# A two-layer attention and long-convolution kernel on one core: 512-column q/k/v products, softmax weights scaled ahead of their transposes, first transfers alternating, raw weights fetched ahead of slots, and a program order planned with other paces

## The chip, the core and the metric

The kernel runs on one core of a Trainium2 chip, as one launch. The metric is the device time of that launch in microseconds (us). The profile names the engines PE (TensorE, with PEld for its weight loads), DVE (VectorE), ACT (ScalarE), POOL (GpSimd) and SP (SyncE, which here only issues transfers).

## What is computed

Two layers of a diffusion backbone over 512 latent tokens and 256 context tokens, width 1024, all in float32. Cut to what matters:

```python
for layer in range(2):
    mod, mod_c = silu(c) @ w_mod + b_mod, silu(c_ctx) @ w_mod + b_mod   # six shifts, scales, gates
    h = rms_norm(x, norm_mix) * (1 + scale1) + shift1                   # h_ctx the same, by mod_c
    q, k, v, hy, g = split(h @ w_in)             # 8 query heads, 2 key/value heads of 128, 1536, 2048
    q, k = rope(head_norm(q)), rope(head_norm(k))
    p = softmax(q @ keys.T * 128**-0.5)          # latents see 256 context and 512 latent keys
    attn = p @ vals
    hyo = long_conv(short_conv(hy)) ...          # by DFT; filters from a small sine MLP
    merged = sigmoid(g_a) * (attn @ w_o_attn) + sigmoid(g_h) * (hyo @ w_o_hyena)
    x = x + gate1 * (merged @ w_out)
    x = x + gate2 * swiglu(rms_norm(x) * (1 + scale2) + shift2)
return rms_norm(x, norm_final)
```

In layer 0 the context tokens pass through everything; in layer 1 only their keys and values are needed.

## The kernel before, in words

Activations lie transposed, as eight tiles of 128 features by 768 tokens (512 latents, then 256 context). Each operand of a large product is kept as two float32r tiles, a high part and the rest, and `mm3` (L233) makes a product of three matmuls: high by high, high by low, low by high. Weights come as raw tiles of 512 KB (`w_load`, L330); ACT copies the high part, DVE subtracts for the low one. Slots are fixed (`SLOTS`): 5 raw, 4 high, 4 low, 37 of 768 columns ("s"; short-lived use is asked for as "t"), 13 of 1024 columns ("f"), 8 PSUM banks ("ps").

**Order.** No engine's order is written by hand. Generators (`job`, `attn_part`, `norm`, ...) yield what their next step needs. `Order` (L65) keeps a clock for each engine, adds a rough cost for every instruction, and lets that generator go on which can and has the lowest priority number. What is emitted is the program order of each engine, and on the chip each engine runs its own row strictly in that order.

**Stages.**

- Front: a filter MLP of three layers (`filter_mlp`, L609), whose seven DVE instructions are emitted with each of its products; 32 float32 products of the conditioning with `wmodf` (`mod_first`, L390), in 16 tiles of 512 KB, which give the columns `mod`; squares of the residual, summed (`Sums`, L466), then `rms` (L486: products with ones, a root on DVE, transposes of `ny`), then `norm` (L511), eight feature tiles, two DVE steps each. `program` (L1217) puts transfers on SP's queue: a tile of `wmodf`, and those of x between them by `X_AT`, then those of the context, then weights.
- Hyena columns (`Hyena.cols`, L797), filters and convolutions (by DFT tables).
- q, k, v by `tok_chunk` (L916): tokens are the stationary side, 256 columns of weights are streamed. k, v and four pairs of query heads are six chunks, each with two weight tiles of 4 x 128 rows by 256 columns.
- Attention by `attn_part` (L1021): a unit is one head and 256 queries. Scores, maximum, exponential with its sum, transposes of the unscaled weights in blocks of 128, product with v into `O`; the reciprocal `ri` is then spread over 128 columns by two transposes, copied by ACT, multiplied into `O` by DVE, and split in high and low. 24 units in layer 0 (16 on latents, 8 on context), 16 in layer 1. Gate products run between them.
- Merge, output projection, feed-forward in four groups. At the end of layer 0 the down projection goes by three parts of 256 tokens (`END`); each part is normed for layer 1 while the next is multiplied.

The model's prices that the change touches:

```python
cost = n / 2400 + 0.003 if n >= 192 else 0.213          # mm, float32r
od.run("DMA" if n > 1 << 16 else q, n / 360e3, ...)      # dma
```

Of the kernel before, what the change touches and what calls it, by code (L numbers as in the profile page):

```python
# [19 lines left out]
P = 128  # L20
# [44 lines left out]
class Order:  # L65
    """Puts the work of several generators into one program order.

    A generator yields what its next step needs: tiles that were written, free
    slots ("tag", n) or Events. Rough costs of the instructions emitted so far
    say when these are there; of the generators that can go on, the one with  # L70
    the lowest priority number does.
    """
# [7 lines left out]
    @staticmethod  # L80
    def span(ap):
        step = ap.ap[0][0]
        lo = ap.offset % step if step else ap.offset
        return ap.tensor.name, lo, lo + 1 + sum((n - 1) * abs(st) for st, n in ap.ap[1:])
# [16 lines left out]
    def run(self, eng, cost, outs, ins, late=0.15, born=None, after=0.0):  # L101
        start = max(self.now[eng], after)
        if born is not None:
            start = max(start, self.born.get(born.tensor.name, 0.0))
        for ap in ins:
            if ap.tensor.name in self.writes:
                start = max(start, self.after(ap, eng))
        for ap in outs:
            start = max(start, self.born.get(ap.tensor.name, 0.0))
        end = start + cost  # L110
        self.now[eng] = end
        for ap in ins:
            n = ap.tensor.name
# [13 lines left out]
    def give(self, tag, i, tile_):  # L127
        self.free[tag].append((self.used.get(tile_.tensor.name, 0.0), i))
# [45 lines left out]
LANES, MORE_LANES = (2, 5), (0, 3)  # L174
# [4 lines left out]
START = 2  # L179
# [8 lines left out]
SLOTS = {"raw": 5, "hi": 4, "lo": 4, "s": 37, "f": 13, "ps": 8}  # L188


def hyena_body(ctx, tc, I, out):
# [7 lines left out]
    # ------------------------------------------------------------- tiles and instructions  # L199
    def new(tag, dt=F32, n=None):  # L200
# [71 lines left out]
    def dma(o, i, eng=None):  # L272
# [4 lines left out]
        od.run("DMA" if n > 1 << 16 else q, n / 360e3, [o], [i], late=2.0, after=od.now[q])  # L277
# [10 lines left out]
    def rsqrt(y, u):  # L288
        """y becomes (u / RS) ** -0.5."""
# [37 lines left out]
    loaded, at = {}, [0, 0]  # L327
    w_here = [Event() for _ in plan]

    def w_load(src, nk, nf, one=False):  # L330
        n = nk * nf
        raw = new("raw")
        if one:
# [5 lines left out]
        loaded[at[1]] = [x.rearrange("p (k f) -> p k f", k=nk) for x in (hi, lo)] + [tiles]  # L339
        w_here[at[1]].set = True  # L340
        raw_n = raw[:, 0:n]
        dma(raw_n.rearrange("p (k f) -> p k f", k=nk), src, nc.sync)
        yield [raw_n]
# [1233 lines left out]
```

## Time and profile before

| | |
|---|---|
| time, median of 3 runs | 2189.53 us (2187.34 to 2191.62) |
| span of the profiled execution | 2187.6 us |
| what lies around the span in that execution | not in the profile; the median stands 1.9 us above the span |
| DMA, mean over the span | 117 GB/s |
| ACT busy | 34% |

The span runs from the first to the last instruction in the trace. A share of busy time is the union of an engine's instructions; matmuls overlap, so a busy PE hides gaps shorter than a matmul's latency. How fast PE really goes is read from the count of matmuls in a stretch without gaps.

### The profile page before, as it was taken

What the parts mean: (1) busy time and instruction counts of PE and PEld (TensorE: products, weight loads), DVE (VectorE), ACT (ScalarE), POOL (GpSimd) and SP (SyncE); (2) the same over time, 40 slices, a digit from 0 to 9 for tenths busy, and PEclk for the clock granted to TensorE, in tenths of its full rate; (3) what the DMA queues carried; (4) which work ended last, traced back from release to release, by engine and by line L of the source; (5) the groups of instructions that cost most, each with busy time, mean ns of one, the idle gap of its engine ahead of it and who ended that gap; (6) DMA issues with size and microseconds to landing.
All of it is one profiled execution on the core that took longest, in us unless ns stands there. A gap on an engine that the chain in (4) does not pass through costs nothing.

```text
span 2187.6 us, 31896 instructions
## 1 busy us (share of the span) xinstructions
PE 2146.5 (98%) x12849; PEld 1888.5 (86%) x12849; DVE 1365.3 (62%) x2510; ACT 744.3 (34%) x1350; POOL 116.8 (5%) x218
## 2 busy tenths in 40 slices
PE   7999999999999999999999999999999999999997
PEld 2889999999888888888888887899888898888887
DVE  5879766665796799733333477766756666434345
ACT  3432234444522421121221334224455443222222
POOL 2111100000100000000000011200001000000000
PEclk9999999999999999999999999999999999999999
DMA  9334521112465257812112232522213433323221
GB/s 327 100 117 151 192 81 46 37 51 80 152 229 183 78 196 239 306 44 74 65 50 82 102 111 91 182 85 73 102 49 121 158 111 99 106 83 111 80 95 57
DMA packets 83060, 256.84 MB, mean 117 GB/s; under 512 B 10668, under 2 KB 15183, under 8 KB 82912
## 3 DMA queue, kind: packets, MB, share of 16 engines
q1 hardware_dynamic: 63840, 197.43, 26.7%
q0 software_dynamic: 19072, 57.36, 8.0%
q8 instruction: 101, 1.65, 0.3%
q14 instruction: 47, 0.39, 0.1%
HBM read 232.07 MB, written 22.68 MB: 116 GB/s over the span
## 4 chain that ended last, share of the span: by engine, by line
PE 92%; DVE 4%; issue 2%; ACT 1%; DMA 1%; POOL 0%; SPq 0%; DVEq 0%; ACTq 0%; POOLq 0%
PE ps L230 89%; PE ps L240 3%; DVE s L250 1%; DVE f L254 1%; ACT s L244 1%; DVE s L254 1%; DMA s<-gated 0%; DVE mx L265 0%; DVE lo L254 0%; DMA s<-in_fw 0%; DMA f<-in_wmodf 0%; ACT hi L244 0%; ACT f L244 0%; POOL s L273 0%; DVE ss L265 0%
## 5 line engine op out<-in xcount | busy, mean ns | idle before, releaser
L230 PE MATMUL ps<-s,hi 128*128 128x512 f32 (+1 forms) x4288 | 1136.2, 353 | 7.5 <-ACT s L244 3.6
L230 PEld LDWEIGHTS ps<-s,hi 128*128 128x128 f32 x4288 | 748.5, 190 | 113.9 <-ACT s L244 4.9
L230 PE MATMUL ps<-s,lo 128*128 128x512 f32 (+1 forms) x2144 | 751.6, 351 | 1.0 <-DVE lo L254 1.0
L230 PEld LDWEIGHTS ps<-s,lo 128*128 128x128 f32 x2144 | 406.5, 190 | 55.5 <-DVE lo L254 1.4
L244 ACT ACTIVATE hi<-raw 128x1024 fp32r<-128x1024 f32 (+2 forms) x272 | 267.3, 994 | 354.1 <-PE ps L230 217.7
L254 DVE TENSOR_TENSOR lo<-raw,hi 128x1024 fp32r<-128x1024 f32 (+2 forms) x272 | 308.0, 1142 | 48.8 <-ACT hi L244 46.8
L230 PE MATMUL ps<-f,hi 128*128 128x512 f32 (+1 forms) x1184 | 297.0, 341 | 0.0
L250 DVE SCALAR_TENSOR_TENSOR s<-s,ps 128x512 f32<-128x512 f32 (+1 forms) x184 | 107.0, 587 | 280.1 <-ACT s L244 150.4
L244 ACT ACTIVATE s<-ps 128x512 f32<-128x512 f32 (+5 forms) x228 | 107.9, 492 | 353.5 <-PE ps L230 273.8
L230 PEld LDWEIGHTS ps<-f,hi 128*128 128x128 f32 x1184 | 205.0, 190 | 25.4
L230 PE MATMUL ps<-f,lo 128*128 128x512 f32 (+1 forms) x592 | 201.4, 340 | 0.0
L230 PE MATMUL ps<-hi,s 128*128 128x256 f32 x1024 | 191.6, 285 | 0.4 <-ACT s L244 0.4
L250 DVE SCALAR_TENSOR_TENSOR s<-ps,mod,s 128x256 f32<-128x256 f32 (+1 forms) x144 | 83.1, 586 | 154.2 <-PE ps L230 154.0
L230 PEld LDWEIGHTS ps<-hi,s 128*128 128x128 f32 x1024 | 162.0, 192 | 0.6 <-ACT s L244 0.6
L230 PE MATMUL ps<-f 128*128 128x256 f32 (+1 forms) x1014 | 145.5, 290 | 7.5 <-DMA f<-in_fw 3.9
L244 ACT ACTIVATE f<-ps 128x512 fp32r<-128x512 f32 (+2 forms) x164 | 90.2, 585 | 170.0 <-PE ps L230 127.2
L230 PE MATMUL ps<-lo,s 128*128 128x256 f32 x512 | 144.9, 283 | 0.0
L230 PEld LDWEIGHTS ps<-f 128*128 128x128 f32 (+1 forms) x1014 | 131.0, 190 | 12.4 <-DVE f L254 4.4
L244 ACT ACTIVATE s<-ps,nb 128x256 f32<-128x256 f32 (+1 forms) x144 | 80.7, 567 | 146.4 <-DVE nb L259 142.5
L244 ACT ACTIVATE s<-s 128x256 f32<-128x256 f32 (+4 forms) x161 | 76.6, 484 | 157.7 <-DVE s L250 125.3
L230 PEld LDWEIGHTS ps<-f,lo 128*128 128x128 f32 x592 | 112.2, 189 | 12.6
L254 DVE TENSOR_TENSOR f<-ps,f 128x512 fp32r<-128x512 f32 (+2 forms) x144 | 90.2, 654 | 41.2 <-ACT f L244 40.2
(119 smaller groups left out, 1858.9 us busy)
## 6 DMA issues: line engine op xcount, KB each, us to landing
raw<-in_w_gu SPq DMA_DIRECT2D x88, 512.0 KB, 3.3
raw<-in_wmodt SPq DMA_DIRECT2D x80, 512.0 KB, 4.3
raw<-in_w_down SPq DMA_DIRECT2D x48, 384.0 KB, 3.1
raw<-in_w_gate SPq DMA_DIRECT2D x32, 512.0 KB, 3.4
raw<-in_w_hy SPq DMA_DIRECT2D x24, 512.0 KB, 4.4
raw<-in_w_qkv SPq DMA_DIRECT2D x24, 512.0 KB, 3.3
raw<-in_w_out SPq DMA_DIRECT2D x24, 512.0 KB, 3.2
f<-in_tab POOLq DMA_DIRECT2D x40, 256.0 KB, 5.6
```

The lines of the kernel that those rows point to most:

```text
L230: nc.tensor.matmul(out=o, lhsT=l, rhs=r, start=start, stop=stop)
L240: nc.tensor.transpose(o, x, ident[0:n, 0:n])
L244: nc.scalar.activation(out=o, in_=i, func=f, **kw)
L250: nc.vector.scalar_tensor_tensor(out=o, in0=a, scalar=s, in1=b, op0=op0, op1=op1)
L254: nc.vector.tensor_tensor(out=o, in0=a, in1=b, op=op)
```

## The change

- `tok_chunk` streams 512 columns. k and v of both heads are one chunk, the queries two chunks of four heads; a weight tile is 2 x 128 rows by 512 columns. A chunk goes through the tokens in two halves of 3 tiles (2 in layer 1's queries), with as many PSUM banks at once, and holds four weight tiles.
- `attn_part`: after the exponential and `ri`, DVE multiplies both weight tiles by `ri`; the two transposes of `ri`, ACT's copy and DVE's product at the end go; ACT and DVE split `O` from PSUM, in a generator of its own.
- Front: a tile of `wmodf` and one of x alternate, then a tile of `wmodf` and one of the context; four weights are asked for after the eighth pair. The first hyena columns of layer 0 take three weights at once. The filter stage is a generator of its own.
- Weights: a raw tile may be fetched when fewer than 6 weights are under way, not only when a high and a low slot are free.
- The model: 0.0135 for 0.003 us per matmul, half the price for small float32 products, 400 for 360 GB/s. Priorities, the number of attention lanes and the placing of gate products differ.

```diff
-LANES, MORE_LANES = (2, 5), (0, 3)
+LANES, MORE_LANES = (2, 10), (4, 5)
-X_AT = (2, 5, 8, 10, 12, 13, 14, 15)
-CONV, SPEC, TURN, ROPE, LANE, HYP, NORM2, LONG, STORE, SPLIT = -7, 1, 4, 2, 4, -7, 2, 3, 3, -5
+FIRST_W, AHEAD = 4, 2
+CONV, SPEC, TURN, ROPE, LANE, HYP, NORM2, LONG, STORE, SPLIT = -3, 3, 4, -1, 4, -10, 4, 3, 4, -5
-MIX = ((2, 0, 1, 0), (0, 1, 0, 0))
-EARLY = (5, 3)
+MIX = ((4, 2, 2, 1), (3, 2, 2, 1))
...
-            cost = n / 2400 + 0.003 if n >= 192 else 0.213
+            cost = n / 2400 + 0.0135 if n >= 192 else 0.213
...
-    def w_load(src, nk, nf, one=False):
+    def w_load(i, src, nk, nf, one=False):
...
+        raw_n = raw[:, 0:n]
+        dma(raw_n.rearrange("p (k f) -> p k f", k=nk), src, nc.sync)
+        yield [raw_n] + ([("f", 1)] if one else [("hi", 1), ("lo", 1)])
...
-            if not all(od.free[tag] for tag in (("f",) if len(plan[at[1]]) > 3 else ("hi", "lo"))):
+            one = len(plan[at[1]]) > 3
+            if not od.free["f"] if one else at[2] >= SLOTS["hi"] + AHEAD:
                 break
...
     def tok_chunk(h, nt, evac):
+        nh = nt // P // 2
         ws = []
+        for half in range(2):
+            yield [("ps", nh)]
+            os = [new("ps") for _ in range(nh)]
+            for kq in range(4):
+                if not half:
+                    ws.append((yield from w_get()))
+                wh, wl, _ = ws[kq]
+                for i, o in enumerate(os):
+                    t = nh * half + i
+                    s = slice(P * t, P * t + P)
+                    for kk in range(2):
+                        k = 2 * kq + kk
+                        yield [h[k][0][:, s], h[k][1][:, s]]
+                        mm3(o, h[k][0][:, s], h[k][1][:, s], wh[:, kk, :], wl[:, kk, :], k == 0, k == KD - 1)
+                if half:
+                    w_done(ws[kq])
...
+        yield [x[:, 0:P * nk] for x in Ps]
...
+        for i in range(2):
+            ts(Ps[i][:, 0:P * nk], Ps[i][:, 0:P * nk], ri[:, i:i + 1], ALU.mult)
...
-        for i in range(2):
-            tr(O[:, 256 + P * i:256 + P * i + P], ri[:, i:i + 1].to_broadcast([P, P]))
-        rb = Ps[0]
-        act(rb[:, 0:256], O[:, 256:512])
-        yield [rb[:, 0:256]]
-        tt(rb[:, 0:256], O[:, 0:256], rb[:, 0:256], ALU.mult)
...
+            act(qh[:, q0:q0 + 256], O)
+            yield [qh[:, q0:q0 + 256]]
+            tt(ql[:, q0:q0 + 256], O, qh[:, q0:q0 + 256], ALU.subtract)
...
         for i in range(16):
+            if i == 8:
+                todo.append((None, None))
             todo.append((None, I["wmodf"][MOD_ORDER[i // 4], i % 4]))
-            todo += [(xs[j][:, 0:SEQ], I["xT"][:, j, :]) for j in range(KD) if X_AT[j] == i]
-        todo += [(xs[j][:, SEQ:TOK], I["ctxT"][:, j, :]) for j in range(KD)]
+            j, part, src = i % KD, *(((0, SEQ), "xT"), ((SEQ, TOK), "ctxT"))[i // KD]
+            todo.append((xs[j][:, part[0]:part[1]], I[src][:, j, :]))
```

Three places of the program order, before and after. In the changed kernel line 230 is 234, 240 is 244, 250 is 254, 254 is 258, 259 is 263 and 261 is 265.

**PE in the front.** `ps<-f,silc` are the products with `wmodf` (two per tile), `ps<-s,f` a layer of the filter MLP, `ps<-ident,s` the transposes that give `mod`, `ps<-ones,s` the sum of the latents' squares, `ps<-ident,ny` its root, `ps<-s,hi` the first hyena columns. Before:

```order
L230 MATMUL ps<-f,silc 2x512 x6
L230 MATMUL ps<-s,f 64x512 x2
L230 MATMUL ps<-f,silc 2x512 x2
L240 MATMUL ps<-ident,s 128x2 x4
L230 MATMUL ps<-f,silc 2x512 x8
L240 MATMUL ps<-ident,s 128x2 x4
L230 MATMUL ps<-f,silc 2x512 x4
L230 MATMUL ps<-ones,s 128x2 x4
```

After:

```order
L234 MATMUL ps<-f,silc 2x512 x6
L234 MATMUL ps<-s,f 64x512 x2
L244 MATMUL ps<-ident,s 128x2 x4
L234 MATMUL ps<-ones,s 128x2 x4
L234 MATMUL ps<-f,silc 2x512 x8
L244 MATMUL ps<-ident,ny 128x128 x4
L234 MATMUL ps<-f,silc 2x512 x4
L234 MATMUL ps<-s,hi 128x512 x2
```

The sum with ones now stands ahead of the last 16 products with `wmodf`, where 14 of them ran before it, and the first columns stand ahead of the last four.

**DVE at the same place.** `f<-ps,fbq` opens the block of the filter MLP's third layer, `s<-s 128x512` adds a square to the latents' sum, `mod` are the columns, `lo<-raw,hi` the low part of a weight, `nv` the first step of the root. Before:

```order
L261 TENSOR_SCALAR f<-ps,fbq 128x512
L261 TENSOR_SCALAR f<-f 128x512
L259 TENSOR_SCALAR f<-f 128x512
L250 SCALAR_TENSOR_TENSOR f<-f 128x512 x3
L261 TENSOR_SCALAR f<-f 128x512
L254 TENSOR_TENSOR s<-s 128x512
L254 TENSOR_TENSOR mod_86<-ps,bmod 128x4
L254 TENSOR_TENSOR mod_87<-ps,bmod 128x4
L254 TENSOR_TENSOR s<-s 128x512 x3
```

After:

```order
L265 TENSOR_SCALAR f<-ps,fbq 128x512
L265 TENSOR_SCALAR f<-f 128x512
L263 TENSOR_SCALAR f<-f 128x512
L254 SCALAR_TENSOR_TENSOR f<-f 128x512 x3
L265 TENSOR_SCALAR f<-f 128x512
L258 TENSOR_TENSOR s<-s 128x512
L258 TENSOR_TENSOR mod_86<-ps,bmod 128x4
L258 TENSOR_TENSOR mod_87<-ps,bmod 128x4
L258 TENSOR_TENSOR lo<-raw,hi 128x1024 x3
L265 TENSOR_SCALAR nv<-ps 128x4
```

The add behind the block is the last of the seven adds now; before, four more came after it.

**DVE at the change of layers.** `acol_12365` and `mod10` (before), `acol_11880` and `mod10` (after) belong to the norm of the second half of the latents, `acol_12429` or `acol_11993` and `mod11` to that of the context; `s_7047` to `s_7054` (before) and `s_6586` to `s_6593` (after) are the feature tiles 0 to 7. Before, the end of the context's norm:

```order
L250 SCALAR_TENSOR_TENSOR s_12455<-s_7053,acol_12429,s_12427 128x256
L250 SCALAR_TENSOR_TENSOR s_12005<-s_12451,mod11_89,s_12004 128x256
L250 SCALAR_TENSOR_TENSOR s_12459<-s_7050,acol_12365,s_12363 128x256
L250 SCALAR_TENSOR_TENSOR s_11999<-s_12415,mod10_88,s_11998 128x256
L250 SCALAR_TENSOR_TENSOR acol_12365<-mod10_88,nmix_74 128x4
L250 SCALAR_TENSOR_TENSOR s_12470<-s_7054,acol_12429,s_12427 128x256
```

After, the start of the context's norm:

```order
L254 SCALAR_TENSOR_TENSOR s_11985<-s_6591,acol_11880,s_11878 128x256
L254 SCALAR_TENSOR_TENSOR s_11542<-s_11969,mod10_88,s_11541 128x256
L254 SCALAR_TENSOR_TENSOR acol_11993<-mod11_89,nmix_74 128x4
L254 SCALAR_TENSOR_TENSOR s_11995<-s_6586,acol_11993,s_11991 128x256
L254 SCALAR_TENSOR_TENSOR s_11998<-s_6587,acol_11993,s_11991 128x256
L254 SCALAR_TENSOR_TENSOR s_11534<-s_11995,mod11_89,s_11533 128x256
```

Before, the latents' tile 2 was finished (`s_11999`) behind the context's norm; now tiles 0 to 4 are finished (`s_11542` is tile 4) ahead of it, and 5 to 7 behind.

More of the change, by code (lines that the diff above doesn't have):

```diff
@@ L78, in __init__, with span, name @@
         self.kept = 0
-    @staticmethod
-    def span(ap):
+    def span(self, ap):
         step = ap.ap[0][0]
         lo = ap.offset % step if step else ap.offset
-        return ap.tensor.name, lo, lo + 1 + sum((n - 1) * abs(st) for st, n in ap.ap[1:])
+        hi = lo + 1 + sum((n - 1) * abs(st) for st, n in ap.ap[1:])
+        return ap.tensor.name, lo, hi
+    def name(self, ap):
+        return self.span(ap)[0]
     def ready(self, ap):
@@ L127, in give @@
     def give(self, tag, i, tile_):
-        self.free[tag].append((self.used.get(tile_.tensor.name, 0.0), i))
+        self.free[tag].append((self.used.get(self.name(tile_), 0.0), i))
     def when(self, needs):
@@ L276, in dma @@
         od.run(q, cost, [], [i], born=o)
-        od.run("DMA" if n > 1 << 16 else q, n / 360e3, [o], [i], late=2.0, after=od.now[q])
+        od.run("DMA" if n > 1 << 16 else q, n / 400e3, [o], [i], late=2.0, after=od.now[q])
     def split(hi, lo, x, *free):
@@ L338, in w_load @@
             hi, lo = tiles[0][:, 0:n], tiles[1][:, 0:n]
[L339 to L343, printed above, removed]
+        loaded[i] = [x.rearrange("p (k f) -> p k f", k=nk) for x in (hi, lo)] + [tiles]
+        w_here[i].set = True
         act(hi, raw_n)
@@ L348, in w_load, with w_more @@
         w_more()
-    def w_more():
-        while at[1] < len(plan) and od.free["raw"]:
-            if not all(od.free[tag] for tag in (("f",) if len(plan[at[1]]) > 3 else ("hi", "lo"))):
+    def w_more(upto=INF):
+        while at[1] < min(len(plan), upto) and od.free["raw"]:
+            one = len(plan[at[1]]) > 3
+            if not od.free["f"] if one else at[2] >= SLOTS["hi"] + AHEAD:
                 break
-            od.spawn(w_load(*plan[at[1]]), 0)
             at[1] += 1
+            at[2] += not one
+            od.spawn(w_load(at[1] - 1, *plan[at[1] - 1]), 0)
     def w_get():
@@ L367, in w_done @@
             drop(*w[2])
+            at[2] -= len(w[2]) > 1
         w_more()
@@ L574, in pair_job @@
         for a, b in spans:
-            yield [("ps", 2)]
-            os = [new("ps")[:, 0:b - a] for _ in range(2)]
+            yield [("ps", len(evacs))]
+            os = [new("ps")[:, 0:b - a] for _ in evacs]
             for k in range(n):
@@ L1296, in program @@
             counts[1].set = False
-            def v_evac(ps, t0):
-                for i in range(2):
-                    split(v[0][t0 + i], v[1][t0 + i], ps[:, 256 * i:256 * i + 256], *[ps] * i)
-                if t0 == 4:
-                    counts[1].hit()
-                yield []
-            yield from tok_chunk(h, TOK, rope_evac(l, 1, rope, kT, counts[0]))
-            yield from tok_chunk(h, TOK, v_evac)
+            yield from tok_chunk(h, TOK, rope_evac(1, rope, [kT], counts, v))
+            counts[1].hit()
             qT = []
@@ L1315, in program @@
                 lane()
-            yield [counts[0]]
-            drop(rope[1][2])
-            for g in range(4):
-                yield [("s", 4)]
-                dst = [(new("s", F32R), new("s", F32R)) for _ in range(2)]
-                qT += dst
-                yield from tok_chunk(h, nt, rope_evac(l, 0, rope, dst, counts[2 + g]))
-                for j in islice(gates, MIX[l][g]):
+            for j in islice(gates, MIX[l][1]):
+                yield from gate_job(l, h, nt, j)
+            od.spawn(last_use(counts[0:1], [rope[1][2]]))
+            for g in range(2):
+                yield [("s", 8)]
+                dst = [[(new("s", F32R), new("s", F32R)) for _ in range(2)] for _ in range(2)]
+                qT += dst[0] + dst[1]
+                yield from tok_chunk(h, nt, rope_evac(0, rope, dst, counts[2 + 2 * g:4 + 2 * g]))
+                for j in islice(gates, MIX[l][2 + g]):
                     yield from gate_job(l, h, nt, j)
```

151 lines of the change are left out of this document (75 added, 76 removed).

## The prediction

> **What bounds the kernel now.** I read the page's head first, then its slices, the chain, stretches without a gap, and last the few places where PE stands still.
>
> ```profile
> span 2187.6 us, 31896 instructions
> PE 2146.5 (98%) x12849; PEld 1888.5 (86%) x12849; DVE 1365.3 (62%) x2510; ACT 744.3 (34%) x1350; POOL 116.8 (5%) x218
> PE   7999999999999999999999999999999999999997
> PE 92%; DVE 4%; issue 2%; ACT 1%; DMA 1%; POOL 0%; SPq 0%; DVEq 0%; ACTq 0%; POOLq 0%
> ```
>
> PE is busy in 98% of the span and is 92% of the chain; only the first and the last slice are below 9. So a part of the change is worth what it takes off PE's row, or off PE's waits at the two ends and the change of layers. DVE at 62% matters where PE waits for it.
>
> The columns of the next view are the stretch, its length, then busy us and instructions of PE, PEld, DVE, ACT and POOL, PE's granted clock, the DMA share and GB/s.
>
> ```profile
> 1437.00:1462.00 25.00, 25.00 (x210) 25.00 (x210) 12.74 (x27) 5.57 (x8) 3.76 (x7) 1.00 0.33 112
> 1900.00:2000.00 100.00, 100.00 (x443) 82.81 (x442) 41.30 (x48) 25.97 (x33) 0.00 (x0) 1.00 0.29 95
> 1464.22 0.87 PE ps L240 x8
> L240 PE MATMUL ps<-ident,ri 128*128 128x128 f32 x80 | 15.2, 271 | 0.0
> ```
>
> The first stretch holds k and v of layer 1, 256-column matmuls alone; the second the feed-forward, 512 columns alone. Some two matmuls reach over the edges of each: 25 / 208 = 0.120 us for 256 columns, 100 / 441 = 0.227 us for 512. Two of the first cost 0.240, so 0.0133 us per pair is cost per instruction. Eight transposes follow at 0.87 / 8 = 0.109 us.
>
> **The sum, part by part, against the span of 2187.6.**
>
> *512 columns.* q, k, v of layer 0 are 6 chunks x 6 token tiles x 8 x 3 = 864 matmuls, of layer 1 288 for k, v and 384 for q: 1536 of 256 columns become 768 of 512. 1536 x 0.120 - 768 x 0.227 = **-10.2 us**, all on the path.
>
> The Trainium skill, TensorE: Matmul & The Clock Gate, section Back-to-back issue gap, gives N / 2.4 + 2.5 ns for a warm matmul; by it a pair would save 2.5 ns and the edit 1.9 us. The stretches above differ with it (13 ns), and the sum goes by them.
>
> *The transposes of `ri`.* 40 units x 2 = the 80 of the row, at 0.109: -8.7; where they stand alone behind a wait less of it counts, by their own row 15.2 us busy with overlap at most. I take **-8.0**.
>
> *Scaling on DVE.* No row shows a tensor by a column of scalars over 768 columns.
>
> ```profile
> L261 DVE TENSOR_SCALAR f<-f 128x512 f32<-128x512 f32 x6 | 2.6, 426 | 0.2
> L254 DVE TENSOR_TENSOR s<-ps,s 128x256 f32<-128x256 f32 x44 | 18.4, 420 | 15.1 <-ACT s L244 10.7 <-PE ps L230 4.0
> 400.00:450.00 50.00, 49.12 (x363) 46.42 (x362) 37.10 (x87) 24.06 (x55) 1.08 (x2) 1.00 0.20 65
> 1500.00:1550.00 50.00, 50.00 (x358) 46.95 (x357) 39.60 (x80) 25.53 (x47) 1.09 (x2) 1.00 0.28 95
> 1725.70 0.38 PE L240 MATMUL ps<-ident,ri 128*128 128x128 f32 x2
> 1727.53 0.96 PE L230 MATMUL ps<-s,hi 128*128 128x512 f32 x2 [1.44 <-ACT s L244]
> ```
>
> It lies between 0.43 us (512 columns) and 1.5 times that, 0.64; I take 0.6, as width counts. 32 units on latents x 2 x 0.6 + 8 on context x 2 x 0.3 = 43 us more DVE, less 40 products of 0.42 = 17: some +26 in about 500 us of attention, where DVE is busy 37 to 40 of 50. That lies beside PE as long as other lanes and gate products stand between: nothing on the path, if that cover holds (a rival, below). ACT loses 40 copies. At the end of layer 1's attention PE waits for the chain behind the last `ri` (1.44 us in the last row); copy and product go from it, and the new order has five tiles of the next product ahead of that need: **-1.5**.
>
> *Front.* The first row is of the chain, the others of the timeline (start, length) and of stretches.
>
> ```profile
> 2.40 4.37 DMA f<-in_wmodf
> 24.82 1.08 PE L230 MATMUL ps<-s,f 64*64 64x512 f32 x4
> 27.98 7.03 PE L230 MATMUL ps<-f,silc 128*2 128x512 f32 x16
> 42.10 0.62 PE L240 MATMUL ps<-ident,ny 128*128 128x128 f32 x4 [0.44 <-DVE ny L250]
> 45.94 1.01 PE L230 MATMUL ps<-ones,s 128*128 128x2 f32 x4 [2.89 <-DVE s L254]
> 50.98 3.78 PE L230 MATMUL ps<-s 64*128 64x256 f32 x8 [4.02 <-DMA s<-in_fw]
> 26.02 0.81 DVE L261 TENSOR_SCALAR f<-ps,fbq 128x512 f32<-128x512 f32 x1 [1.89 <-PE ps L230]
> 29.97 0.43 DVE L261 TENSOR_SCALAR f<-f 128x512 f32<-128x512 f32 x1
> 51.06 2.35 DVE L254 TENSOR_TENSOR lo<-raw,hi 128x1024 fp32r<-128x1024 f32 x2
> 54.19 0.74 DVE L250 SCALAR_TENSOR_TENSOR s<-s,mod 128x512 fp32r<-128x512 f32 x1
> 25.00:30.00 5.00, 5.00 (x17) 1.02 (x16) 3.77 (x7) 1.61 (x3) 0.00 (x0) 1.00 1.03 403
> 45.00:50.00 5.00, 1.01 (x4) 0.93 (x4) 4.66 (x11) 2.10 (x3) 1.50 (x3) 0.58 1.10 328
> 55.00:60.00 5.00, 5.00 (x14) 3.87 (x14) 4.84 (x9) 3.09 (x6) 0.00 (x0) 0.55 0.31 106
> ```
>
> Before, PE works through to 42.7 and then waits 2.9 and 4.0 us; from 45.8 to 59.5 its clock is half, so that the columns, begun at 54.7, lose 2.3 us more. Counted as if they ran at 0.227 from their start, they start at 57.0.
>
> After, the same instructions stand ahead on PE up to the MLP's third layer, which ends at 25.9 again; tile 7 of `wmodf` lands, with 5.9 MB behind the first tile at 403 GB/s, at 6.8 + 14.6 = 21.4, and PE takes it at some 23, in time. But the last add of the squares stands behind the MLP's block on DVE, 26.0 to 30.4. Add at 31.0, PE idle from 26.3 to 31.1: a **new wait of 4.8 us**. Behind it stand the 16 products left, every column and all of PE. Then: ones to 32.1; 8 products (2 x 0.43 us each, 16 pieces in 7.0) to 39.0; `ny`, for which DVE had from 32.1 with 3 x 1.2 for weights and 2.0 for the root, to 39.6; ACT's copy 0.6, and 0.7 + 0.7 + 0.7 us of norm: tile 0 at 42.5. PE: 4 products to 43.0, tile 0 (9 x 0.227 = 2.0) to 45.1, 4 products to 48.5, transposes, tiles 1 and 2 to 53.0, transposes to 53.4. Tile 3 waits for the last `mod` and two steps (55.4), then tiles 3 to 7 take 10.2 us: 65.7, with the filter's own products (two rows like that at 50.98, 1.7 at full clock), ones and `ny` 69.9. Before, with the same work: 57.0 + 72 x 0.227 = 16.3, and 2.0 = 75.3. Gain 5.4 if the clock holds; I take 2 us for half a clock behind the idle 4.8 (before, it lost 2.3 behind 2.9 and 4.0): **-3.5**, between +1 and -8.
>
> The bytes: 13.9 MB, constants counted, now stand up to the last tile of `wmodf` instead of 10.6; it lands at 6.8 + 13.4 / 0.403 = 40, and PE takes it after 45. Hidden by 5 us.
>
> The Trainium skill has the rule, in the same page, section What's actually happening: the gate looks at free-running windows of 3.4 us. The clock of this trace agrees (half from 45.8 to 59.5, four such windows); whether 4.8 us idle trip it hangs on where the windows fall.
>
> *Change of layers.*
>
> ```profile
> 1291.43 0.41 DVE L254 TENSOR_TENSOR s<-s 128x256 f32<-128x256 f32 x1
> 1304.68 0.61 PE L230 MATMUL ps<-ones,s 128*128 128x2 f32 x4 [3.23 <-DVE s L254]
> 1315.41 0.67 PE L230 MATMUL ps<-s,hi 128*128 128x512 f32 x1 [3.04 <-DVE s L250]
> 1313.68 0.48 DVE L250 SCALAR_TENSOR_TENSOR s<-s,acol 128x256 f32<-128x256 f32 x1
> 1314.08 0.48 DVE L250 SCALAR_TENSOR_TENSOR s<-s,mod 128x256 fp32r<-128x256 f32 x1
> ```
>
> DVE steps follow at 0.40. Before, PE waits at the context's ones, then at tile 2 until the context's norm is through, and from 1315.4 has six tiles left (6 x 6 x 0.227 = 8.2, and 1.7 for the filter): 1325. After, PE takes a tile ahead of ones. From the add at 1291.4, with which both orders reach the same state, DVE has 34 steps of 0.40, two roots of 1.8 and two short ones up to tile 4: 1309.5. Tile 5 stands 17 steps further, 1316.3, and three tiles and the filter end at 1322. Gain 3, of which I count **-2.5**: the wait moves and does not go.
>
> *The rest.* Raw tiles ahead of slots and the q, k, v weights, one raw tile for one as before, meet stretches without a wait (1900 to 2000): nothing, since 4 weights in front of PE cover them; without that cover a weight costs DVE's 1.2 and ACT's 1.1. The smaller pieces of ACT in `tok_chunk` are hidden likewise (25 of 50). The model's paces move PE nearer to the time that the model gives DVE. I take **+2** for waits of that kind in attention, from 0 to +10 in the forecast's own range.
>
> Sum: -10.2 - 8.0 - 1.5 - 3.5 - 2.5 + 2 = -23.7, span 2163.9; the median of the runs stands 1.9 above the span, so about **2165**. 0.2% (4.4 us) is what a measurement can tell.
>
> **Rivals.**
>
> 1. *The waits eat the ends.* Front and change of layers give nothing, since DVE holds PE there as before: only the columns and transposes count, -18.2, and +3 in attention: 2174. For it: the new wait behind the MLP's block. Chance 0.16.
> 2. *The front pays in full.* If no clock is lost and the columns run on from 48.5 without the wait for tile 3, -8 instead of -3.5, and attention adds no wait instead of +2: 2158. Chance 0.14.
> 3. *The fixed cost is not per instruction.* -1.9 instead of -10.2: 2173. The page named above would have it so; against it stand 441 and 208 matmuls. Chance 0.03.
> 4. *Slower: the scaling stands on PE's row.* Between a unit's exponential and its first transpose stand now the reciprocal (0.2) and two scalings, about 1.4 us. If the lanes do not cover it, 40 x 1.4 = 56 us against -25.7: 2220. It decides from 25.7 / 40 = 0.64 us uncovered per unit. Against it: DVE is idle a quarter of that stage, and as many gate products as before (12 and 13 for 11 and 13) lie between the units; for it: with truer paces the model leaves less to spare, and DVE's real steps are not priced anew. Half covered, 28 us, is 2192. Chance 0.09, of which 0.06 end slower than before by over 0.2% and 0.02 within.
>
> **How the numbers follow.** Forecast 2165 (own range 2157 to 2172), chance 0.58. Range 2150 to 2180: it takes in rivals 1 to 3 and leaves out the fourth and tails. Faster 0.92, within 0.2% 0.02, slower 0.06.
>
> **What will show it.** In the changed profile: 512-column matmuls of q, k, v at 0.227; no `ident,ri` row; PE idle some 5 us between 26 and 31 with `ones` waiting for DVE, the last half clock earlier or gone, columns from about 43; at 1300 less a wait at tile 5 for DVE. Wrong would be the forecast by a row of PE waits for DVE ahead of transposes in attention, or by a front without that wait.

## The result and the profile after

| | median of the runs, us | lowest to highest | span of the profiled run, us |
|---|---|---|---|
| before | 2188.91 | 2187.34 to 2191.62 | 2187.6 |
| changed | 2169.32 | 2166.94 to 2170.03 | 2167.5 |

The row of before holds one run more than the table ahead of the prediction. The ratio of changed to before is 0.9901, with a 95% interval of 0.9887 to 0.9915. By the medians the change makes the kernel 19.6 us faster; the forecast was 2165 with a range of 2150 to 2180.

The head of the changed kernel's page, its PE row in 40 slices, and the shares of the chain:

```profile
span 2167.5 us, 30309 instructions
PE 2129.8 (98%) x12001; PEld 1837.0 (85%) x12001; DVE 1388.0 (64%) x2550; ACT 732.1 (34%) x1336; POOL 117.1 (5%) x218
PE   8999999999999999999999999999999999999997
PE 88%; DVE 7%; issue 3%; ACT 1%; DMA 1%; POOL 0%; SPq 0%; DVEq 0%; ACTq 0%; POOLq 0%
```

PE still sets the end. There are 848 fewer matmul records, and DVE is 23 us busier. The chain has more DVE in it than before (7% for 4%).

A matmul's busy time overlaps the next one's, so I account for PE in another way: for each matmul of the trace, the time to the start of the next, less its pace (0.227 us for 512 columns, 0.120 for 256, 0.109 for a transpose, and so on). What is left over is PE's waits, half clock included (half clock: stretches in which the profile shows a granted TensorE clock of 0.5, so that the same matmuls take longer). Summed by stretch, in us:

| stretch of the span | what runs there | before | changed | no scalings | square first | tables | old front | none ahead | old prices | both repairs |
|---|---|---|---|---|---|---|---|---|---|---|
| 0 to 100 | front | 19.6 | 16.2 | 16.5 | 13.7 | 16.4 | 24.7 | 17.1 | 14.1 | 15.9 |
| 100 to 250 | layer 0, columns and filters | 2.7 | 3.3 | 3.2 | 2.5 | 3.4 | 2.4 | 3.4 | 9.1 | 2.6 |
| 250 to 600 | layer 0, q, k, v and attention | 5.7 | 12.2 | 7.3 | 10.6 | 8.3 | 10.8 | 16.7 | 24.7 | 8.4 |
| 600 to 1250 | merge, feed-forward | 3.4 | 3.5 | 3.4 | 3.4 | 3.5 | 3.5 | 4.0 | 5.8 | 3.5 |
| 1250 to 1350 | change of layers | 12.4 | 9.6 | 8.1 | 12.9 | 13.7 | 8.1 | 8.0 | 12.8 | 12.0 |
| 1350 to 1780 | layer 1, q, k, v and attention | 9.6 | 6.7 | 5.4 | 7.7 | 6.8 | 7.6 | 17.3 | 18.9 | 6.8 |
| 1780 to the end | feed-forward, last norm | 7.3 | 8.6 | 7.8 | 8.7 | 8.6 | 8.7 | 7.2 | 7.9 | 7.8 |
| sum | | 60.8 | 60.1 | 51.7 | 59.4 | 60.6 | 65.8 | 73.6 | 93.3 | 56.9 |

(The last seven columns are experiments 2, 4, 5, 9, 10, 8 and 12 below.) PE's own work, counted by the same paces, fell from 2114.8 to 2095.9: 18.9 us, which is 1536 x 0.120 - 768 x 0.2267 = 10.2 and 80 x 0.109 = 8.7. The waits fell by 0.7 only. So **nearly the whole gain is work taken off PE**; the waits only changed places: 3.4 us less in the front, 2.8 less at the change of layers and 2.9 less in layer 1's attention, 6.5 more in layer 0's and 1.3 more in the last stretch.

What PE waits for in the changed kernel (line and tile, engine waited for, us in total, times, longest):

```profile
PE ps L234 <- ACT s L248: 5.9, 6, 1.6
PE ps L234 <- DVE mod L258: 4.9, 1, 4.9
PE ps L234 <- DMA f<-in_fw: 3.8, 1, 3.8
PE ps L244 <- DVE f L258: 2.9, 2, 2.1
PE ps L234 <- DVE s L258: 2.5, 3, 1.6
PE ps L234 <- DVE s L254: 2.4, 1, 2.4
PE ps L244 <- DVE ny L254: 2.0, 1, 2.0
PE ps L244 <- ACT s L248: 1.9, 2, 1.5
PE ps L234 <- DVE lo L258: 1.9, 1, 1.9
```

The 4.9 is the predicted one of the front; the `DVE s L254` is the predicted one at the change of layers; `DVE lo`, at 262, was not foreseen. `DVE f L258` in front of transposes has the look of the sign that I had named as one against the forecast; its 2.1, at 1513, is for the rope of the queries, and stays as long when the scalings are left out (experiment 2). Timeline of the front, first PE, then DVE (start, length, tiles, count, idle time before with what ended it):

```profile
25.96 0.40 PE L244 MATMUL ps<-ident,s 2*128 2x2 f32 x4
31.27 1.84 PE L234 MATMUL ps<-ones,s 128*128 128x2 f32 x8 [4.91 <-DVE mod L258]
33.04 8.61 PE L234 MATMUL ps<-f,silc 128*2 128x512 f32 x16
41.58 0.65 PE L244 MATMUL ps<-ident,ny 128*128 128x128 f32 x4
45.68 0.73 PE L234 MATMUL ps<-s,hi 128*128 128x512 f32 x2
...
26.15 0.81 DVE L265 TENSOR_SCALAR f<-ps,fbq 128x512 f32<-128x512 f32 x1 [1.08 <-PE ps L234]
30.10 0.43 DVE L265 TENSOR_SCALAR f<-f 128x512 f32<-128x512 f32 x1
30.44 0.68 DVE L258 TENSOR_TENSOR s<-s 128x512 f32<-128x512 f32 x1
```

The last square-add runs at 30.44 behind the filter MLP's block. `ones` need the sum; the profile names `mod` only because that add ended last, right behind it. The clock is half from 29.4 to 36.2, so `ones` take 1.84 and the 8 products behind them (16 pieces) 8.61, where 8 took 7.03 before. Hence the columns start at 45.7, later than the 42.5 that I had worked out (2 us for half clock apart), but at full clock. Before, they started at 54.7, at half clock:

```profile
54.69 1.22 PE L230 MATMUL ps<-s,hi 128*128 128x512 f32 x2
```

At the change of layers:

```profile
1309.32 0.73 PE L234 MATMUL ps<-s,hi 128*128 128x512 f32 x1 [2.41 <-DVE s L254]
```

Five tiles of six matmuls each stand ahead of it: the wait is at tile 5, for DVE's norm, as foreseen. From 1250 to 1350 PE now stands idle for 4.7 us, where it was 6.4 (busy 95.34 and 93.58 of 100); the other 1.0 of the table's 2.8 is half clock, two windows there before (1305.3 and 1315.6) and one now.

### The profile page after: what moved, and what is told of

It is laid out like the page before. It is cut to its first block, busy times and chain, and to the rows that moved or that the text cites. A ratio compares the mean times of both kernels' runs of the same rounds, so it can differ in the third digit from the quotient of the medians.

```text
span 2167.5 us, 30309 instructions
## 1 busy us (share of the span) xinstructions
PE 2129.8 (98%) x12001; PEld 1837.0 (85%) x12001; DVE 1388.0 (64%) x2550; ACT 732.1 (34%) x1336; POOL 117.1 (5%) x218
## 4 chain that ended last, share of the span: by engine, by line
PE 88%; DVE 7%; issue 3%; ACT 1%; DMA 1%; POOL 0%; SPq 0%; DVEq 0%; ACTq 0%; POOLq 0%
PE ps L234 85%; PE ps L244 3%; DVE f L258 2%; DVE s L254 2%; DVE s L258 1%; DVE lo L258 1%; ACT s L248 1%; DVE mx L269 0%; DMA s<-in_rcos 0%; DVE ss L269 0%; DVE s L263 0%; DVE rq L258 0%; DMA f<-in_wmodf 0%; ACT hi L248 0%; DVE rq L254 0%
## 5 line engine op out<-in xcount | busy, mean ns | idle before, releaser
L258 DVE TENSOR_TENSOR lo<-raw,hi 128x1024 fp32r<-128x1024 f32 (+2 forms) x272 | 309.1, 1142 | 100.0 <-ACT hi L248 97.6
L254 DVE SCALAR_TENSOR_TENSOR s<-s,ps 128x512 f32<-128x512 f32 (+1 forms) x184 | 107.0, 586 | 267.6 <-ACT s L248 143.7
L248 ACT ACTIVATE s<-ps 128x256 f32<-128x256 f32 (+5 forms) x234 | 107.7, 482 | 314.9 <-PE ps L234 236.4
L254 DVE SCALAR_TENSOR_TENSOR s<-ps,mod,s 128x256 f32<-128x256 f32 (+1 forms) x144 | 82.9, 585 | 152.0 <-PE ps L234 151.7
L234 PE MATMUL ps<-hi,s 128*128 128x512 f32 x512 | 165.2, 395 | 0.0
L248 ACT ACTIVATE f<-ps 128x512 fp32r<-128x512 f32 (+3 forms) x184 | 91.3, 538 | 137.4 <-PE ps L234 85.5
L234 PEld LDWEIGHTS ps<-hi,s 128*128 128x128 f32 x512 | 97.0, 189 | 19.5
L458 DVE CUSTOM_DVE_ANT_0 raw<-raw,f 128x1024 f32<-128x1024 f32 x80 | 97.9, 1224 | 23.7 <-DMA raw<-in_wmodt 21.9
L269 DVE TENSOR_REDUCE mx<-ps 128x1 f32<-128x512 f32 (+1 forms) x104 | 68.4, 684 | 61.0 <-PE ps L234 61.0
L258 DVE TENSOR_TENSOR f<-ps,f 128x512 fp32r<-128x512 f32 (+2 forms) x144 | 90.7, 654 | 24.9 <-ACT f L248 24.1
```

The lines of the kernel that those rows point to most:

```text
L234: nc.tensor.matmul(out=o, lhsT=l, rhs=r, start=start, stop=stop)
L248: nc.scalar.activation(out=o, in_=i, func=f, **kw)
L254: nc.vector.scalar_tensor_tensor(out=o, in0=a, scalar=s, in1=b, op0=op0, op1=op1)
L258: nc.vector.tensor_tensor(out=o, in0=a, in1=b, op=op)
L269: nc.vector.tensor_reduce(out=o, in_=a, op=op, axis=AX.X)
L458: nc.vector.tensor_tensor_reduce(out=junk[:, 0:D], in0=raw, in1=cond[s], scale=1.0, scalar=0.0, op0=ALU.mult, op1=ALU.add, accum_out=mraw[ ...
```

## Experiments

Each expectation was written before its run. Ratios are against the kernel before, run on the same chip. Waits are counted as in the table above.

### 1. 256-column halves in the changed order

```diff
-                        mm3(o, h[k][0][:, s], h[k][1][:, s], wh[:, kk, :], wl[:, kk, :], k == 0, k == KD - 1)
+                        mm6(o, h[k][0][:, s], h[k][1][:, s], wh[:, kk, :], wl[:, kk, :], k == 0, k == KD - 1)
...
+    def mm6(o, lh, ll, rh, rl, start, stop):
+        for l, r, a, b in ((lh, rh, start, False), (lh, rl, False, False), (ll, rh, False, stop)):
+            for c in (slice(0, 512),) if a or b else (slice(0, 256), slice(256, 512)):
+                nc.tensor.matmul(out=o[:, c], lhsT=l, rhs=r[:, c], start=a, stop=b)
...
```

> The changed kernel, in the same order on every engine, but of each q, k, v product of 512 columns the 22 matmuls between the first and the last of its 24 are two of 256 columns: 32 products x 22 = 704 instructions more (768 matmuls / 24 = 32 products). Theory A (what a pair saves is a cost of each instruction, 2 x 0.120 - 0.227 = 0.0133 us): span 2167.5 + 9.4 = 2176.9. Rival (a fixed cost of only some 2.5 ns, the Trainium skill's formula): + 1.8 = 2169.3. PE's waits stay as they are, within 1 us, in both.

Median 2175.43, ratio 0.9942 (0.9925 to 0.9958): 0.41% of 2189 or 9.0 us above the changed kernel by the ratios, 6.1 by the medians. Stretches of q, k, v without a gap, first in the changed kernel, then in this one (busy us and instructions of PE and PEld lead):

```profile
272.00:284.00 12.00, 12.00 (x55) 9.94 (x54) 3.21 (x3) 3.67 (x5) 0.00 (x0) 1.00 0.28 89
```

```profile
270.00:285.00 15.00, 15.00 (x124) 14.86 (x123) 4.96 (x5) 4.78 (x6) 0.00 (x0) 1.00 0.27 82
```

12 / 53 = 0.226 us for a whole one; in the second stretch 118 halves follow each other at a mean of 0.120, with four whole ones between. The pace is a cost of each instruction, and work rose by 9.4. The span rose by 5.7 only (2173.2 for the 2176.9 of theory A), because the waits, which I had expected to stay within 1 us, fell from 60.1 to 56.6; 2.4 of that is at 262, where the wait was shorter and no half clock followed. Theory A holds for the work, and the rival's 1.8 is below every measure of the time. The Trainium skill (TensorE: Matmul & The Clock Gate, Back-to-back issue gap) has 2.5 ns as the fixed part of an isolated matmul; here it is 13 ns, and the measurement decides.

### 2. The scalings left out

```diff
-            ts(Ps[i][:, 0:P * nk], Ps[i][:, 0:P * nk], ri[:, i:i + 1], ALU.mult)
+            x = Ps[i][:, 0:P * nk]
+            od.run("DVE", 0.065 + size(x) * 0.0006, [x], [x])
```

> The changed kernel in the same order, with the 80 scalings of the softmax weights left out on DVE (the attention's output is then not normalised). Between 250 and 600 us PE stands still 12.1 us in the changed kernel against 5.6 before. Theory A (the scalings lie beside PE; the new waits have other causes: rope tables, weights, the order): span 2166 to 2168, DVE 40 us less busy. Rival (the scalings make the new waits of layer 0's attention): those 6.5 us go, span about 2161.

Median 2164.03, ratio 0.9883 (0.9866 to 0.9900), span 2158.8. Their price in the changed kernel, from the groups kept apart by shape (busy us, mean ns):

```profile
L263 DVE TENSOR_SCALAR s<-s,ri 128x768 f32<-128x768 f32 x64 | 36.9, 619 | 1.2
L263 DVE TENSOR_SCALAR s<-s,ri 128x256 f32<-128x256 f32 x16 | 4.9, 351 | 0.3
```

I had priced them 0.6 and 0.3. Layer 0's waits fell by 4.9 and layer 1's by 1.3; of the first, 1.5 is a half clock behind the wait at 262 (below), which this run did not draw. So **the scalings cost 4 to 5 us**, neither nothing nor all of the 6.5. Both kernels have the same order on PE, so they can be set against each other matmul by matmul: from 275 to 500 the difference is under 0.1 us, from 500 to 600 it is 3.3, and of layer 1's 1.3 nearly all lies between 1650 and 1700. The cover held in most of the attention and leaked towards the end of each layer's. The wait at 262 and one of 1.5 at 439 are still there without the scalings. The span fell by 8.7, more than that and more than the rival's 6.5: half-clock time up to 2140 us was 6.8 us here for 17.1.

### 3. The old way to normalise, in the changed kernel

```diff
-        for i in range(2):
-            ts(Ps[i][:, 0:P * nk], Ps[i][:, 0:P * nk], ri[:, i:i + 1], ALU.mult)
...
-        drop(*Ps)
-        yield list(pts[-1]) + vs(nk // 2 - 1)
+        yield list(pts[-1]) + [ri] + vs(nk // 2 - 1)
         pv(nk // 2 - 1)
+        for i in range(2):
+            tr(Ob[:, 256 + P * i:256 + P * i + P], ri[:, i:i + 1].to_broadcast([P, P]))
...
-            act(qh[:, q0:q0 + 256], O)
+            rb = Ps[0][:, 0:256]
+            act(rb, Ob[:, 256:512])
+            yield [rb]
+            tt(rb, O, rb, ALU.mult)
...
+            act(qh[:, q0:q0 + 256], rb)
```

> The changed kernel with the old way to normalise: 80 transposes of ri, the copy and the product behind them, no scaling. Theory A (the two parts of this term hold as priced: 80 x 0.109 = 8.7 of PE and 1.5 of the chain at the end of layer 1's attention, and the scalings cost nothing): span 2176 to 2178. Rival (the scalings cost 6.5 us of waits in layer 0, so the net of this edit is only some 3 us): 2170 to 2172.

Both missed: median 2218.75, ratio 1.0133 (1.0118 to 1.0148). The weights `Ps` hold their two tiles until the end of a unit again, the planner sets another order, and PE loses 40 us between 400 and 500, half clock included. PE's projections of 512 columns in that stretch, in the changed kernel and in this one:

```profile
L234 PE MATMUL ps<-s,hi 128*128 128x512 f32 x112 | 35.4, 397 | 0.0
```

```profile
L234 PE MATMUL ps<-s,hi 128*128 128x512 f32 x27 | 8.8, 406 | 0.0
```

With a quarter of the projections between the units, too little covers the chains of softmax and rope. That the held tiles keep the planner from placing gate products is argued from the code, not shown. As an undo this run is no measure of the part alone.

### 4. The last square-add ahead of the filter MLP's block

```diff
-    def filter_mlp(L, np_):
+    def filter_mlp(L, np_, first=None):
...
+            if i == 2 and first:
+                yield [first]
             ts(an, m[0:np_, 0:L], fbq[0:np_, 0, i:i + 1], ALU.add, fbq[0:np_, 1, i:i + 1], ALU.mult)
...
-        od.spawn(filter_mlp(SEQ, P), -1)
+        od.spawn(filter_mlp(SEQ, P, sums[0].done), -1)
```

> The changed kernel with the filter MLP's third layer put behind the latents' last square-add on DVE. Theory A (PE's 4.9 us wait at 26 us is made by that order alone, and 1.6 us of half clock behind it): ones run at about 26.5, the first column starts 4 to 6 us earlier than 45.7, span 2162 to 2164. Rival (behind it stands another: ny's root waits on DVE behind the MLP block, or a wmodf tile lands late): the wait moves to the ny transposes or the products, span 2166 to 2168.

Median 2168.73, ratio 0.9902 (0.9887 to 0.9916). PE's timeline at the front:

```profile
25.56 1.05 PE L234 MATMUL ps<-ones,s 128*128 128x2 f32 x8
27.70 3.15 PE L234 MATMUL ps<-f,silc 128*2 128x512 f32 x4 [1.09 <-DMA f<-in_wmodf]
31.77 0.65 PE L244 MATMUL ps<-ident,ny 128*128 128x128 f32 x4 [0.91 <-DVE ny L254]
32.35 7.03 PE L234 MATMUL ps<-f,silc 128*2 128x512 f32 x16
39.31 0.74 PE L234 MATMUL ps<-s,hi 128*128 128x512 f32 x2
```

`ones` run at 25.56 and the columns start 6.4 us earlier: the order of two pieces on DVE made the wait. Then the rival has its share: the next `wmodf` tile is late by 1.1 and `ny` by 0.9, so that the front's waits fell by 2.5 and not by 4.9; part of the 6.4 is only order, since six products, not four, now stand behind the first column tile. The change of layers took 3.3 back, with half clock from 1304.8 to 1315.0 (one window, 1309.4 to 1312.8, in the changed kernel). The span, 2166.3, is the rival's; by the times alone this repair can't be told from nothing.

### 5. One low half ahead of the rope tables

What happens at 262 in the changed kernel, on DVE and PE, and in stretches (PE's granted clock stands ahead of the last two columns):

```profile
260.13 2.77 DVE L258 TENSOR_TENSOR f<-s,gqk 128x256 f32<-128x256 f32 x8 [8.01 <-DMA s<-in_rcos]
262.82 1.22 DVE L258 TENSOR_TENSOR lo<-raw,hi 128x1024 fp32r<-128x1024 f32 x1
...
264.09 0.50 PE L234 MATMUL ps<-lo,s 128*128 128x512 f32 x1 [1.90 <-DVE lo L258]
```

```profile
260.00:265.00 5.00, 3.10 (x14) 2.27 (x13) 3.91 (x9) 0.00 (x0) 0.00 (x0) 0.99 0.03 13
265.00:270.00 5.00, 5.00 (x17) 3.93 (x16) 0.85 (x2) 1.53 (x5) 0.00 (x0) 0.66 0.35 107
```

DVE stands 8 us for the transfer of a rope table, with a weight's low half behind it in its row; PE waits for that, and then runs 3.4 us at half clock.

```diff
         tabs_ = [new("f") for _ in range(2)]
+        yield [x[:, 0:512] for x in src]
         for w in range(2):
```

> The changed kernel with one DVE instruction moved: the low half of one k, v weight (lo<-raw,hi, 1.22 us) stands ahead of the eight products that build the rope tables, and not behind them. In the changed kernel DVE stands 8.0 us for the transfer of the table (rcos) with that weight behind it, and PE waits 2.06 us for the weight at 261.8. Theory A (that place in DVE's row makes the wait): the wait at 262 goes, and any half clock right behind it; span 2167.5 - 2.1 to - 3.8 = 2163.7 to 2165.4. Rival (the next weight's low half, still behind the tables, is as late): the wait comes 4 us later, span unchanged within 1 us.

The wait is gone, and so is the half clock behind it (waits from 250 to 600: 8.3 for 12.2). The time is not theory A's (a span of 2163.7 to 2165.4) but the same as without the repair: median 2169.77, ratio 0.9907 (0.9892 to 0.9922), span 2167.9. In the profiled run 4.1 us went at the change of layers, half clock from 1293.6 to 1297.0 and 1307.3 to 1317.5. The cause of the wait is shown; a gain in time from this repair alone is not.

### 6. Dead `ri` transposes

```diff
-            O = new("ps")[:, 0:256]
+            Ob = new("ps")
+            O = Ob[:, 0:256]
...
         pv(nk // 2 - 1)
+        for i in range(2):
+            nc.tensor.transpose(Ob[:, 256 + P * i:256 + P * i + P], ri[:, i:i + 1].to_broadcast([P, P]), ident)
```

> The changed kernel in the same order, with the 80 transposes of ri put back on PE as dead work (they write the unused half of O's bank, nothing reads them). Theory A (they lie on the path at PE's own pace): 80 x 0.109 = 8.7, less what falls into waits: PE's work + 8.7, span 2174.5 to 2176.5. Rival (they fill waits, so that the edit's 8.0 was too much): under 2172.

Median 2177.27, 8.0 above the changed kernel (ratio 0.9942, 0.9928 to 0.9957); span 2173.9 with 8.7 more work and 2.2 less waits, with 13.7 us of half clock up to 2140 for 17.1. The profiled span lies 0.6 below theory A's range, the spans of the four runs (2173.2 to 2177.2) all above the rival's: the transposes lay on the path, at about what I had counted.

### 7. The scaling alone, in the kernel before

The edit is that of 3 the other way round, in the kernel before.

> The kernel before with this part of the change alone: softmax weights scaled ahead of the transposes, no ri transposes, copy and product; 256-column q, k, v, the old prices, lanes and order of the front. Theory A (the scaling by itself brings 8.7 of PE work, costs 3 to 5 us in waits as in the run without scalings): before's span 2187.6 - 3 to - 6, 2182 to 2185. Rival (the order was tuned to the old paces and falls apart with the new needs, as when the old way was put into the new order): over 2190.

Median 2208.78, ratio 1.0086 (1.0071 to 1.0101): slower than before by 19 us. Work fell by 8.7, waits rose from 60.8 to 87.9. Three rows of what PE waits for in all, then PE and DVE where it is worst:

```profile
PE ps L230 <- DVE f L254: 10.0, 4, 5.2
PE ps L240 <- DVE s L259: 5.2, 3, 2.6
PE ps L240 <- DVE f L254: 2.7, 2, 1.5
...
1532.47 2.19 PE L240 MATMUL ps<-ident,s 128*128 128x128 f32 x8 [2.59 <-DVE s L259]
...
1531.70 1.15 DVE L259 TENSOR_SCALAR s<-s,ri 128x768 f32<-128x768 f32 x2
1536.88 1.15 DVE L259 TENSOR_SCALAR s<-s,ri 128x768 f32<-128x768 f32 x2
1537.95 1.28 DVE L254 TENSOR_TENSOR f<-ps,f 128x512 fp32r<-128x512 f32 x2
```

PE waits for a unit's scaling in front of its transposes: that is the mechanism of my fourth rival, but only 5.2 us of the 27 are such waits. 12.7 are waits for DVE's `f` tiles (3.3 in the kernel before), in front of which, as at 1536.88, scalings stand in DVE's row as well, and half clock took 58.0 us up to 2140, for 20.5 before. How the 27 us divide between the scalings and the order that the planner set around them is not settled. The changed kernel has the same scalings without a wait of PE that names them, so the order around them decides at least that part.

### 8 and 11. The prices alone

```diff
-            cost = n / 2400 + 0.0135 if n >= 192 else 0.213
+            cost = n / 2400 + 0.003 if n >= 192 else 0.213
...
-        od.run("DMA" if n > 1 << 16 else q, n / 400e3, [o], [i], late=2.0, after=od.now[q])
+        od.run("DMA" if n > 1 << 16 else q, n / 360e3, [o], [i], late=2.0, after=od.now[q])
```

> The changed kernel with the planner's old prices: 0.003 a matmul in place of 0.0135, four passes for all float32 matmuls, 360 in place of 400 GB/s. The instructions are the same, their order is not. Theory A (the truer prices give PE a better cover: with PE taken for too fast, other work is put in late): more waits, span 2168 to 2180, chiefly in attention and the front. Rival (the other numbers of the order carry it, the prices are worth nothing): 2164 to 2170.

(The two passes for small float32 matmuls go back to four as well.) And the other way round in the kernel before:

> The kernel before with the new prices alone (0.0135 a matmul, two passes for small float32 matmuls, 400 GB/s). The instructions are the same, their order is not. Theory A (truer prices help in any order): PE's waits under 60.8, span under 2186. Rival (each set of hand-set numbers fits its own prices only; the prices alone break the old order as the old prices broke the new one): span over 2195.

The changed kernel with old prices: median 2205.36, ratio 1.0075 (1.0058 to 1.0092), 36 us slower, more than either theory gave (theory A, more waits, has the sign). The kernel before with new prices: 2252.16, ratio 1.0281 (1.0266 to 1.0296), waits 124.2. Each set of hand-set numbers fits its own prices. In the changed kernel with old prices, between 500 and 600, transposes wait 10.4 us and there are 46 projections of that kind where the changed kernel has 88:

```profile
L243 PE MATMUL ps<-ident,s 128*128 128x128 f32 x120 | 19.1, 291 | 10.4 <-ACT s L247 8.8 <-DVE s L257 1.6
L233 PE MATMUL ps<-s,hi 128*128 128x512 f32 x46 | 15.0, 405 | 0.0
```

```profile
L234 PE MATMUL ps<-s,hi 128*128 128x512 f32 x88 | 28.1, 399 | 0.0
```

### 9. The first transfers in the old order

```diff
+X_AT = (2, 5, 8, 10, 12, 13, 14, 15)
...
-            if i == 8:
-                todo.append((None, None))
             todo.append((None, I["wmodf"][MOD_ORDER[i // 4], i % 4]))
-            j, part, src = i % KD, *(((0, SEQ), "xT"), ((SEQ, TOK), "ctxT"))[i // KD]
-            todo.append((xs[j][:, part[0]:part[1]], I[src][:, j, :]))
+            todo += [(xs[j][:, 0:SEQ], I["xT"][:, j, :]) for j in range(KD) if X_AT[j] == i]
+        todo += [(xs[j][:, SEQ:TOK], I["ctxT"][:, j, :]) for j in range(KD)]
```

> The changed kernel with the first transfers in the old order (wmodf tiles first, latents between them from the third on, context last; no raw weights among them). The planner sets another order behind it. Theory A (the alternating order brings what the front gained, 3.3 us of PE's waits up to 100 us): PE's waits up to 100 us go back to about 19.6 from 16.3, span 2169 to 2172. Rival (the front's gain comes from other parts of the change, prices or order): waits there stay within 1 us of 16.3.

Median 2176.75, ratio 0.9939 (0.9917 to 0.9961); waits up to 100 us 24.7. Theory A in its sign; the size is over it (it gave 19.6 for the waits and at most 2172 for the span, which is 2172.8), since the columns lose their place behind the first `ny`. The edit also takes the four raw weights out of the front's transfers, so the two aren't told apart:

```profile
44.09 0.65 PE L245 MATMUL ps<-ident,ny 128*128 128x128 f32 x4 [2.04 <-DVE ny L255]
47.70 0.99 PE L235 MATMUL ps<-ones,s 128*128 128x2 f32 x4 [2.96 <-DVE acol L255]
62.10 0.69 PE L245 MATMUL ps<-ident,ny 128*128 128x128 f32 x2 [5.63 <-DVE ny L255]
```

### 10. No raw weights ahead of slots

```diff
-FIRST_W, AHEAD = 4, 2
+FIRST_W, AHEAD = 4, 0
```

> The changed kernel with no raw weights fetched ahead of free slots (limit 4 in place of 6 fetched weights). Theory A (as predicted, the early fetch meets stretches without a wait and is worth nothing): PE's waits within 3 us of 60.1, span 2164 to 2171. Rival (PE waits for weights, lo or hi, without it): a row of waits for DVE lo or ACT hi of over 4 us, span over 2172.

Median 2184.75, ratio 0.9975 (0.9964 to 0.9987): 15 us slower than the changed kernel, and theory A falls. But the rival has only the time right: PE hardly waits for a weight (`DVE lo` 1.8 in all). It waits in both attentions (34.0 us there for 18.9), for softmax and rope, with fewer gate products between. Between 1640 and 1690, changed kernel, then this one:

```profile
L234 PE MATMUL ps<-s,hi 128*128 128x512 f32 x61 | 19.7, 402 | 0.8 <-ACT s L248 0.8
L244 PE MATMUL ps<-ident,s 128*128 128x128 f32 x64 | 8.8, 273 | 0.0
```

```profile
L234 PE MATMUL ps<-s,hi 128*128 128x512 f32 x29 | 10.0, 418 | 3.4 <-DVE f L258 1.2 <-ACT s L248 1.2 <-DVE s L258 1.1
L244 PE MATMUL ps<-ident,s 128*128 128x128 f32 x70 | 11.3, 295 | 4.1 <-ACT s L248 3.9 <-DVE f L258 0.2
```

### 12. Both repairs

The edits of 4 and 5 together.

> The changed kernel with both repairs: the filter MLP's third layer behind the last square-add, and one weight's low half ahead of the rope tables. Theory A (the two waits are apart and both repairs add up in PE's waits outside half-clock windows: 2.6 at the front, 2.1 at 262): median 3 to 5 us under the changed kernel's, 2164 to 2166. Rival (what is gained is lost again at the change of layers or by the clock windows): 2167 to 2170.

Median 2164.53 (2162.36 to 2165.78, all four below the changed kernel's lowest), ratio 0.9879 (0.9864 to 0.9893), waits 56.9. Theory A by the times, 4.8 us under the changed kernel, and the fastest of the kernels that compute everything. That the two repairs add up is not shown: the profiled run, the slowest of the four, has 3.8 of it in layer 0's attention; the front shows 0.3, with two half-clock windows there where experiment 4 drew one, and the change of layers gives 2.4 back.

## Why the prediction was right, step by step

The mechanism held: the two terms that take work off PE are nearly the whole gain, and put back one by one (experiments 1 and 6) they cost 14.1 of the 19.6 us by the medians. Among the waits, errors of both signs offset each other, and that the sum came so near is in part luck.

- **512 columns, -10.2: right.** The paces are 0.226 and 0.120, and the halves put 9.4 us of work back for 704 of the 768 pairs. The product as I wrote it, with 0.227, gives 10.0; 10.2 is with the unrounded 0.2267. (Rivals 2 and 3 are added up a microsecond too low: their terms give 2159 and 2174.)
- **`ri` transposes, -8.0: right.** Put back as dead work they cost 8.0 in the medians, 6.4 in the profiled span.
- **Scaling hidden: right in kind, too cheap.** DVE's durations were near (0.62 and 0.35 us for 0.6 and 0.3), but the cover leaks 4 to 5 us. Together with the wait at 262, attention's waits are the term that was mis-sized: I took +2 with up to +10; measured are +6.5 in layer 0 and -1.3 in layer 1 beside the end chain, +5.2.
- **End of attention, -1.5: right.** The wait of 1.44 behind the last `ri` is gone, and PE has no wait at the end of that attention now.
- **Front, -3.5: right in the sum,** 19.6 to 16.2. The new wait is 4.91 for 4.8 foreseen, and half clock came right with it. The columns started at 45.7, 1.2 behind the 42.5 and the 2 us that I took for half clock; against that, the stop of 2 us that I had in front of tile 3 did not come (PE shows no idle time over 0.25 us from 31.3 to 100). Without the alternating order and the weights among it the front waits 8.5 more.
- **Change of layers, -2.5: right in place,** the wait at tile 5 for DVE's norm. Of the 2.8 from 12.4 to 9.6, PE's idle time is 1.8. The rest hangs on half clock, and is luck: the same stretch took 8.0 to 8.1 in experiments 2, 9 and 10 and 12.0 to 13.7 in 4, 5 and 12, with no more idle time (4.1 to 4.7).
- **Early raw weights, 0: wrong as a price.** The text said that stretches without a wait make them worth nothing. In the changed order they are worth 15 us, and where they are left out fewer gate products lie in attention (29 for 61 in the rows of experiment 10). Reading whether PE waits for weights was the wrong question; what the planner does with the room was the one to ask.
- **q, k, v weights "meet stretches without a wait": wrong at one place,** 262, where a low half stands behind a table's transfer on DVE: 1.9 us and, in some runs, 1.5 of half clock.
- **The slower rival did not come.** Its wait exists: with the scaling alone the old order falls 19 us behind, and 5.2 us of that are PE's waits for a scaling.

The sum was -23.7 on the span, the measured -20.1: 3.2 of the difference is attention, 1.3 the last stretch of the table, which had no term, and the other terms give 0.9 of it back.

The number of attention lanes, the priorities and the placing of gate products were not undone one by one; what each is worth stays open.

## What to carry to other kernels

Work taken off the engine that bounds a kernel adds up as counted: in PE's work, columns and transposes came out within a microsecond of instructions times pace. Waits don't: here each part of the change that sets the planner another order cost 7 to 63 us when it was undone or done alone (experiments 3 and 7 to 11), so a part's worth in waits is only defined together with the prices and hand-set numbers around it. Look in the row of each in-order engine for an instruction that waits for a transfer with something urgent behind it; the repair of experiment 5 moved one such piece, that of experiment 4 an urgent piece that stood behind a block that was not.

## What the runs showed of the hardware

The half clock comes in stretches of 3.4 us or multiples, on a grid that runs on through the whole execution: by the trace's clock record of the changed kernel up to 2140 us it starts at 29.4, 264.9, 1309.4 and 1797.5, and the distances from the first are 69.0, 375.0 and 518.0 times 3.413 us. The Trainium skill (TensorE: Matmul & The Clock Gate, What's actually happening) says that the windows are free-running, and the trace agrees; its "≥1 idle window" for the drop is too strict here, since a wait of 1.9 us at 262 was enough. The same wait drew a half clock in the changed kernel and in experiment 6, and none in 2, 4 and 9. On each run's own grid, it lay inside one step of 3.413 us in the first two (0.7 to 2.6 and 0.7 to 2.5 us after the step's start) and reached over a step's edge in the other three (by 0.07 us only in 4). That is not the whole condition: waits of 1.8 us inside a step at 1519 in experiment 1 and at 547 in experiment 10 drew none. Half-clock time up to 2140 us was 17.1 us in the changed kernel, 6.8 in experiment 2 and 27.3 in experiment 5. At half clock PE loses about half of that where it has work: 8 products that ran 3.2 us of their time at half clock took 8.61 for 7.03. The four runs of experiment 2, one kernel, have spans of 2158.8 to 2165.7 us with granted clocks of 0.996 to 0.993. So the span moves by some us with no change in the code, and a repair of 2 us can't be judged by one profiled run: the waits have to be read stretch by stretch.
